# Moving the seven separately carried rows of a Winograd convolution from a store to a load

## The chip, the cores and the metric

The kernel runs on one core of a Trainium2 chip. The metric is the device time of one execution in microseconds (us). A measurement of this kernel is the median of several runs.

## What is computed

A 3x3 convolution with zero padding of one pixel, over 16 images of 64 channels and 64x64 points, to 128 output channels, all in float32. Cut to what matters, the reference is:

```python
x_pad = np.pad(x, ((0, 0), (0, 0), (1, 1), (1, 1)), mode='constant')
# for every image b, output channel co, input channel ci, and kh, kw in 0..2:
output[b, co] += weight[co, ci, kh, kw] * x_pad[b, ci, kh:kh+h, kw:kw+w]
```

The input is 16.8 MB, the weights 0.3 MB, the output 33.6 MB.

## The kernel before

**Tiling.** Images are taken in eight pairs, p = 0 to 7: the 64 channels of two images fill the 128 partitions, so that one pair is a tile of 128 partitions by 64 rows by 64 columns of float32 (16 KB in each partition, 2 MB in all). Every pair is computed in two halves of 32 output rows. For each half, `transforms` (L135) makes float16 sums, differences and outer differences of rows (`sums` L110, `diffs` L117, `outers` L124), on VectorE for the very first half and on GpSimd for all others, two halves ahead of their use. `cast` (L130) makes a float16 copy of 17 rows on ScalarE, one half ahead. TensorE then runs 54 matmuls of 64 by 128 weights on up to 512 columns (L170), into eight PSUM tiles. ScalarE copies some of them out (L192, L253), and VectorE adds and subtracts the rest into the output tile (L247, L249, L251).

**Homes.** Tiles in SBUF have fixed places. `X_HOME` (L49) gives the place of each input pair: pairs 0, 1 and 2 in slots s0, s1 and s2, pairs 3 and 4 side by side in the double slot "d", pair 5 in s2 again, pairs 6 and 7 in "d" again. `O_HOME` (L50) gives that of the two output images of each pair; pairs 0, 3 and 6 (`BOTH`, L51) use a double tile and are stored by one transfer of 4 MB (L207), the others by one transfer of 2 MB for each image (L216).

**Transfers.** All of them are issued by SyncE (SP in the profile), in the order of the program, on one queue that feeds 16 DMA engines. A transfer over 128 partitions gives each of the 16 engines eight partitions, so eight packets (16 for a double tile), one for each partition and tile, and a record of four bytes at its end, which counts its completion. The order is: weights (L59); pair 0 in two pieces, pair 1, pair 2 (all L67, from `load`, L62); pairs 3 and 4 together (L81); then, as computation finishes, the stores of pairs 0 and 1, the load of pair 5, the stores of pair 2, the load of pair 6, the store of pair 3, the load of pair 7, the stores of pairs 4, 5, 6 and 7. `NEXT_LOADS` (L53) places the loads. SyncE waits at each store for VectorE and ScalarE to have written the tile, at each late load for GpSimd and ScalarE to have read the slot's old contents.

**The seven rows.** `FEW = 5, 1, 7` (L52) names pair 5, image 1, seven rows. In `store` (L204) this one image of the sixth pair is carried in three transfers instead of one: rows 0 to 56 from all 128 partitions (L213), rows 57 to 63 from partitions 0 to 123, and rows 57 to 63 from partitions 124 to 127. The second and third have 1792 bytes in each partition. In the trace their 128 packets lie on four of the 16 DMA engines, 32 on each. Every other transfer of the program lies evenly on all 16.

Of the kernel before, what the change touches and what calls it, by code (L numbers as in the profile page):

```python
# [15 lines left out]
def kernel(  # L16
# [12 lines left out]
    nc = tc.nc  # L29
    B, CI, H, W = x.shape  # L30
    CO = weight.shape[0]
# [4 lines left out]
    keep = tc.keep_in_program_order  # L36
    x_rows = x.rearrange("b c h w -> (b c) h w")
# [11 lines left out]
    X_HOME = [0, 1, 2, ("d", 0), ("d", 1), 2, ("d", 0), ("d", 1)]  # L49
    O_HOME = ["b", (3, 4), (0, 1), "b", (3, 4), (0, 1), "b", (2, 3)]  # L50
    BOTH = (0, 3, 6)  # L51
    FEW = 5, 1, 7  # L52
    NEXT_LOADS = {(1, 1): 5, (3, 0): 6, (4, 0): 7}  # L53

    def home(k, name):
        return slots.tile([128, H, W], F32, tag=f"s{k}", name=name)
# [3 lines left out]
    xs = {}  # L60

    def load(p, cuts=((0, H),)):  # L62
        if X_HOME[p] in range(5):
            xs[p] = home(X_HOME[p], "xs")
        for lo, hi in cuts:
            keep(
                nc.sync.dma_start(  # L67
                    xs[p][:, lo:hi, :], x_rows[128 * p : 128 * p + 128, lo:hi, :]
                )
            )  # L70

    two = slots.tile([128, 2, H, W], F32, tag="d", name="two")
    for p in range(NP):
        if X_HOME[p] not in range(5):
            xs[p] = two[:, X_HOME[p][1], :, :]

    load(0, ((0, 34), (34, H)))
    load(1)
    load(2)
    rows = x_rows[128 * 3 : 128 * 5, :, :].rearrange("(g p) h w -> p g h w", g=2)  # L80
    keep(nc.sync.dma_start(two, rows))  # L81
# [116 lines left out]
    def outputs(p):  # L198
        if O_HOME[p] == "b":
            both = slots.tile([128, 2, H, W], F32, tag="b", name="both")  # L200
            return both, [both[:, b2, :, :] for b2 in range(2)]
        return None, [home(k, "ot") for k in O_HOME[p]]

    def store(p, both, ots):  # L204
        if p in BOTH:
            pair = out[2 * p : 2 * p + 2, :, :, :].rearrange("b c h w -> c b h w")
            keep(nc.sync.dma_start(pair, both))  # L207
            return
        for b2 in range(2):
            parts = [(0, CO, 0, H)]  # L210
            if (p, b2) == FEW[:2]:
                at = H - FEW[2]
                parts = [(0, CO, 0, at), (0, 124, at, H), (124, 4, at, H)]  # L213
            for c, n, lo, hi in parts:
                keep(
                    nc.sync.dma_start(  # L216
                        out[2 * p + b2, c : c + n, lo:hi, :], ots[b2][c : c + n, lo:hi, :]
                    )
                )

    for n, (p, h) in enumerate(halves):
        if n + 2 < len(halves):
            tr[halves[n + 2]] = transforms(nc.gpsimd, *halves[n + 2])
        if h == 0:
            both, ots = outputs(p)
# [28 lines left out]
        if h == 1:  # L254
            store(p, both, ots)
# [32 lines left out]
```

## Time and profile before

| what | value |
|---|---|
| median of 3 runs | 127.15 us (126.87 to 127.34) |
| the profiled execution: its own time | 127.13 us |
| the profiled execution: its span | 125.4 us |
| last matmul group ends | 102.44 us |
| last store issued | from 103.18 us on |
| HBM read / written | 17.07 MB / 33.55 MB |
| mean DMA rate over the span | 405 GB/s |
| granted TensorE clock, mean | 0.917 |

The span is what the profile covers, from its first to its last instruction; the execution's own time holds 1.7 us more around it. All times of instructions and packets below are in us from the start of the span. The page of the profile shows for each engine how busy it was in 40 equal slices of 3.1 us; for the DMA line a digit of 9 means that the 16 DMA engines were busy for 90% of the slice or more. The view of windows gives the same for stretches that one chooses, with the mean rate in GB/s. A DMA share of 1.01 or 1.02 stands for "all 16 engines": successive packets of an engine overlap by some 4 ns.

### The profile page before, as it was taken

The numbers are of one execution on the slowest core, as the hardware profiler recorded it, in microseconds if no ns is written. First come the engines' busy times: TensorE is split into PE (matmuls) and PEld (weight loads), VectorE is DVE, ScalarE is ACT, GpSimd is POOL, SyncE is SP. The second block draws the span as 40 slices with busy tenths as digits, with TensorE's granted clock in tenths as the row PEclk, the third lists the DMA queues.
The fourth block names the chain that finished last, engine by engine and source line by source line (L and its number), as shares of the span: only waits on it lengthen the run. The fifth ranks groups of instructions, "written<-read, shape, count | busy, mean of one in ns | idle before, by whom it ended". The sixth has DMA issues, their size and how long they took to land.

```text
span 125.4 us, 2343 instructions
## 1 busy us (share of the span) xinstructions
PE 95.6 (76%) x873; PEld 48.9 (39%) x873; DVE 66.8 (53%) x104; ACT 85.4 (68%) x150; POOL 90.5 (72%) x52
## 2 busy tenths in 40 slices
PE   0349999999999999999999999999999960000000
PEld 0223555555455555555555555555555520000000
DVE  0199658393939476574939394765749390000000
ACT  4458598989797988989897979789898930000000
POOL 2209999999999999999999999999999300000000
PEclk9999999999999999999999999999999996555555
DMA  4999999999999999999999999999999999999971
GB/s 132 371 453 423 434 424 439 423 335 418 434 431 429 426 434 418 423 429 434 416 439 424 423 423 423 418 431 434 423 424 423 433 416 443 423 429 444 418 335 47
DMA packets 3827, 50.78 MB, mean 405 GB/s; under 512 B 360, under 2 KB 488, under 8 KB 744
## 3 DMA queue, kind: packets, MB, share of 16 engines
q1 hardware_dynamic: 3816, 50.63, 96.2%
q8 instruction: 7, 0.11, 0.3%
q14 instruction: 4, 0.03, 0.1%
HBM read 17.07 MB, written 33.55 MB: 404 GB/s over the span
## 4 chain that ended last, share of the span: by engine, by line
PE 76%; DMA 2%; DVE 2%; POOL 1%; DVEq 0%; ACT 0%; issue 0%
PE acc L170 75%; DMA w_raw<-in_weight_dram 2%; DVE ss L114 1%; DVE ot L251 1%; POOL w L87 1%; DVEq L283 0%; DVE th L141 0%; DVE Wt L142 0%; PE wp L102 0%; ACT g0h L139 0%; DVEq L142 0%
## 5 line engine op out<-in xcount | busy, mean ns | idle before, releaser
L170 PEld LDWEIGHTS <-Wt 64*128 64x128 f16 x864 | 48.0, 96 | 48.5 <-issue 3.0
L192 ACT COPY ut<-acc 128x512 f32<-128x512 f32 x96 | 48.7, 612 | 4.4 <-PE acc L170 4.4
L170 PE MATMUL acc<-xh,Wt 64*128 64x504 f16 (+3 forms) x384 | 46.2, 372 | 0.0
L170 PE MATMUL acc<-ss,Wt 64*128 64x504 f16 (+1 forms) x192 | 24.8, 392 | 2.3 <-DVE ss L114 2.3
L170 PE MATMUL acc<-ee,Wt 64*128 64x504 f16 (+1 forms) x192 | 26.4, 377 | 0.0
L247 DVE TENSOR_TENSOR ot<-acc,ut 128x512 f32<-128x512 f32 x20 | 12.9, 686 | 20.0 <-ACT ut L192 15.8
L114 POOL TENSOR_TENSOR ss<-xs 128x1024 f16<-128x1024 f32 x7 | 16.6, 2366 | 4.7 <-DMA xs<-in_x_dram 4.7
L127 POOL TENSOR_TENSOR ee<-two 128x1024 f16<-128x1024 f32 x8 | 19.0, 2378 | 0.0
L114 POOL TENSOR_TENSOR ss<-two 128x1024 f16<-128x1024 f32 x8 | 19.0, 2369 | 0.0
L127 POOL TENSOR_TENSOR ee<-xs 128x1024 f16<-128x1024 f32 x7 | 16.6, 2376 | 0.0
L253 ACT COPY ot<-acc 128x512 f32<-128x512 f32 x20 | 10.7, 589 | 5.5 <-PE acc L170 5.5
L170 PE MATMUL acc<-dd,Wt 64*128 64x504 f16 (+1 forms) x96 | 13.9, 392 | 0.0
L247 DVE TENSOR_TENSOR both<-acc,ut 128x512 f32<-128x512 f32 x12 | 7.7, 686 | 11.0 <-ACT ut L192 7.9
L251 DVE TENSOR_TENSOR ot<-ut,acc 128x512 f32<-128x512 f32 x20 | 12.8, 682 | 0.2
L249 DVE TENSOR_TENSOR ot<-acc,ut 128x512 f32<-128x512 f32 x20 | 12.8, 680 | 0.0
L121 POOL TENSOR_TENSOR dd<-two 128x512 f16<-128x512 f32 x8 | 10.3, 1287 | 0.0
L121 POOL TENSOR_TENSOR dd<-xs 128x512 f16<-128x512 f32 x7 | 10.0, 1423 | 0.0
L132 ACT CAST xh<-two 128x1088 f16<-128x1088 f32 x8 | 9.3, 1157 | 0.0
L132 ACT CAST xh<-xs 128x1088 f16<-128x1088 f32 x8 | 9.2, 1145 | 0.0
L253 ACT COPY both<-acc 128x512 f32<-128x512 f32 x12 | 6.4, 589 | 3.5 <-PE acc L170 3.5
L251 DVE TENSOR_TENSOR both<-ut,acc 128x512 f32<-128x512 f32 x12 | 7.7, 683 | 0.1
L249 DVE TENSOR_TENSOR both<-acc,ut 128x512 f32<-128x512 f32 x12 | 7.7, 680 | 0.0
(23 smaller groups left out, 14.9 us busy)
## 6 DMA issues: line engine op xcount, KB each, us to landing
out_dram<-ot SPq DMA_DIRECT2D x9, 2048.0 KB, 18.5
out_dram<-both SPq DMA_DIRECT2D x3, 4096.0 KB, 22.5
xs<-in_x_dram SPq DMA_DIRECT2D x3, 2048.0 KB, 16.2
two<-in_x_dram SPq DMA_DIRECT2D x1, 4096.0 KB, 28.4
two<-in_x_dram SPq DMA_DIRECT2D x2, 2048.0 KB, 23.1
out_dram<-ot SPq DMA_DIRECT2D x1, 1824.0 KB, 24.3
xs<-in_x_dram SPq DMA_DIRECT2D x1, 1088.0 KB, 5.4
xs<-in_x_dram SPq DMA_DIRECT2D x1, 960.0 KB, 7.4
```

The source lines that it names most:

```text
L87: keep(nc.gpsimd.tensor_copy(w16[:, 0, :], w_raw))
L114: keep(eng.tensor_add(t, v[:, j : j + 16, 0, :], v[:, j : j + 16, 1, :]))
L121: keep(eng.tensor_sub(t, v[:, j : j + RB, 1, :], v[:, j : j + RB, 0, :]))
L127: keep(eng.tensor_sub(t, xs[p][:, r - 1 : r + 15, :], xs[p][:, r + 1 : r + 17, :]))
L132: keep(nc.scalar.copy(t, xs[p][:, C_ROW[h] : C_ROW[h] + 17, :]))
L170: nc.tensor.matmul(tiles[b2][:, lo:hi, c_lo:c_hi], Wt[p0 : p0 + 64, wi, kw, :], src[p0 : p0 + 64, first : last + 1 : step, c_lo + kw - 1 : ...
L192: keep(nc.scalar.copy(ut, tiles[b2]))
L247: keep(nc.vector.tensor_add(ov[b2][:, jg : jg + RB, 1, :], pg2[b2], ug[b2]))
L249: keep(nc.vector.tensor_add(ov[b2][:, jf : jf + RB, 0, :], pf1[b2], uy[b2]))
L251: keep(nc.vector.tensor_sub(ov[b2][:, jf : jf + RB, 1, :], ux[b2], pf2[b2]))
L253: keep(nc.scalar.copy(ov[b2][:, jg : jg + RB, 0, :], pg1[b2]))
```

## The change

The split in three transfers is taken from the store of the sixth pair's second image and given to the load of the third pair (p = 2), as rows 0 to 56 over all partitions, rows 57 to 63 over partitions 0 to 123, and rows 57 to 63 over partitions 124 to 127. The store becomes one transfer of 2 MB. The number of transfers, the bytes and the number of packets stay as they are; so does every instruction of the compute engines, in kind and order.

```diff
-    FEW = 5, 1, 7
+    FEW = 2, 7
...
     def load(p, cuts=((0, H),)):
         if X_HOME[p] in range(5):
             xs[p] = home(X_HOME[p], "xs")
-        for lo, hi in cuts:
-            keep(
-                nc.sync.dma_start(
-                    xs[p][:, lo:hi, :], x_rows[128 * p : 128 * p + 128, lo:hi, :]
-                )
-            )
+        parts = [(0, 128, lo, hi) for lo, hi in cuts]
+        if p == FEW[0]:
+            at = H - FEW[1]
+            parts = [(0, 128, 0, at), (0, 124, at, H), (124, 4, at, H)]
+        for c, n, lo, hi in parts:
+            r = 128 * p + c
+            keep(nc.sync.dma_start(xs[p][c : c + n, lo:hi, :], x_rows[r : r + n, lo:hi, :]))
...
         for b2 in range(2):
-            parts = [(0, CO, 0, H)]
-            if (p, b2) == FEW[:2]:
-                at = H - FEW[2]
-                parts = [(0, CO, 0, at), (0, 124, at, H), (124, 4, at, H)]
-            for c, n, lo, hi in parts:
-                keep(
-                    nc.sync.dma_start(
-                        out[2 * p + b2, c : c + n, lo:hi, :], ots[b2][c : c + n, lo:hi, :]
-                    )
-                )
+            keep(nc.sync.dma_start(out[2 * p + b2, :, :, :], ots[b2]))
```

## The prediction

> **What bounds the kernel now.** I read the page first: the slices, the queues, the chain.
>
> ```profile
> PE   0349999999999999999999999999999960000000
> DMA  4999999999999999999999999999999999999971
> q1 hardware_dynamic: 3816, 50.63, 96.2%
> ```
>
> TensorE stops at slice 33, the DMA engines go on to slice 39. The chain of waits ends in a store of VectorE's last tile at 103 us and gives 75% to the matmuls; but the 22 us behind that are transfers alone. SyncE's own waits and the chain end tell why:
>
> ```profile
> SPq L283 <- DMA out_dram<-ot: 9.9, 3, 4.8
> ...
> SPq L283 <- DMA out_dram<-both: 9.6, 1, 9.6
> ...
> 102.44 0.68 DVE ot L251
> 103.12 0.60 DVEq L283
> ```
>
> After the last store is issued (103.18) the core only waits for stores issued before. So the queue is the bound, and the question is when its last engine is done. The view of windows at the end:
>
> ```profile
> 104.00:116.00 12.00, 0.00 (x0) 0.00 (x0) 0.00 (x0) 0.00 (x0) 0.00 (x0) 0.52 1.01 433
> ...
> 120.00:121.00 1.00, 0.00 (x0) 0.00 (x0) 0.00 (x0) 0.00 (x0) 0.00 (x0) 0.50 0.77 328
> 121.00:122.00 1.00, 0.00 (x0) 0.00 (x0) 0.00 (x0) 0.00 (x0) 0.00 (x0) 0.50 0.65 279
> 122.00:123.00 1.00, 0.00 (x0) 0.00 (x0) 0.00 (x0) 0.00 (x0) 0.00 (x0) 0.50 0.35 147
> 123.00:124.00 1.00, 0.00 (x0) 0.00 (x0) 0.00 (x0) 0.00 (x0) 0.00 (x0) 0.50 0.08 33
> ```
>
> The share falls from 1 to 0 over four microseconds: the engines end at different times, and the last one sets the end. No view lists engines, so I took the trace's packet records (start, duration, bytes) and joined each to the one that starts 4 ns before its end; that gives 16 unbroken chains. Where two packets end within a few ns the join can swap two engines; the counts of 1792-byte packets show it for one of the four engines below. What I read from the chains:
>
> - A 16384-byte packet takes 607 ns from start to start, one of 14592 bytes (57 rows) 541, one of 1792 bytes 70. There is no gap on any engine from 2 us to its end.
> - The four engines with 32 packets of 1792 bytes ("the four") end at about 122.0 to 122.9 (the swapped one), 122.60, 123.20 and 123.38; the other twelve between 120.18 and 124.17, the last two at 124.07 and 124.17. Then 1.2 us of end work make the span, 1.7 more the execution's 127.13, which is the median of the runs (127.15) but for 0.02.
> - The pieces of seven rows are what brings the four near the end: at the end of the big piece of that store they stand at 100.9 to 101.7, the two slowest others at 104.6 and 104.7.
>
> **The change part by part.**
>
> *Work for each engine.* Removed from the store and added to the load are the same packets. On each of the four: 32 x 70 = 2.24 us more, 8 x (607 - 541) = 0.53 us less; on each of the twelve 0.53 less. Over the whole run each engine's sum stays. Between the third pair's load (about 18 us) and the sixth pair's store (about 101 us) the four are now 1.71 us later than before and the twelve 0.53 earlier, 2.24 apart. That a read of 1792 bytes costs as a write, no row shows; the reads at hand go as fast as writes (8704 bytes 324 ns, so 27 bytes/ns, as for 16384), so I take 70; bounds 70 and 89, what a read packet of 2304 bytes took: 32 x 19 = 0.6 us more on the four.
>
> *Does an engine run dry?* The twelve reach each later transfer 0.53 us earlier. A packet starts 1.0 us after its issue (weights: 0.74, first packet 1.74). What was issued but not moved is the cover. Least at the store of pair 1 (34.14 + 1.0): moved are 35.14 us x 391 GB/s = 13.74 MB, issued before are 14.98 MB (weights 0.29, seven units of 2.097), so 1.24 MB or 2.9 us at 432 GB/s. Next least is the first store: 10.78 - 9.33 MB, 3.4 us. So 0.53 is covered; if it weren't, the gap would cost at most 0.53 on fast engines, which end up to 4 us before the last.
>
> *SyncE.* Two issues move ahead of the double load, at 0.3 to 0.45 us each: it is issued at 3.9 instead of 3.07, and served at 18. Nothing.
>
> *Readers of the rows.* GpSimd's sums of the second half of pair 2 and ScalarE's copy of it get two more waits, at 27.7 and 31.1. The pieces land at about 18.4 + 1.7 = 20.1. Nothing. Late loads of the four (pair 6, pair 7) come 1.7 us later: pair 7 on them at 82 to 84.5, GpSimd needs it at 86.46, nothing; and a delay in GpSimd has 7.6 us of queue (3.3 MB left at 104.18) before it touches the end.
>
> *Changeovers from loads to stores.* Here the order matters.
>
> ```profile
> 24.00:26.00 2.00, 2.00 (x22) 1.00 (x19) 0.82 (x2) 2.00 (x5) 2.00 (x3) 1.00 1.02 434
> 26.00:29.00 3.00, 3.00 (x32) 1.59 (x30) 2.90 (x5) 2.34 (x5) 3.00 (x2) 1.00 0.99 322
> 29.00:33.00 4.00, 4.00 (x42) 2.05 (x40) 2.15 (x4) 3.56 (x7) 4.00 (x3) 1.00 1.01 430
> ```
>
> Where the double load ends and the first store begins, the rate falls by a quarter with all engines "busy". In the chains fifteen engines end the load between 28.2 and 28.7 and lose 0.3 to 1.0 us each. The sixteenth shared its time with an instruction fetch at 21.25 (each of seven such fetches costs its engine about 1.3 us), was still loading when the others stored, had one packet of 2.15 us, and ended at 31.18: the end of its load before (18.21) + 16 x 0.607 + 1.3 would be 29.2, so it lost 1.95, some 1.0 more than the worst of the others. It is the engine that ends last, at 124.17. Again at pair 6's load: most engines end it at about 67.3 without loss; those that end later lose 1.13 (end 71.21), 0.56 (69.47), 0.24 and 0.19 (69.3, 68.9). At pair 5's and pair 7's loads late engines lose 0 to 0.5, without order. So reading late, beside others' writes, has cost 0 to 1.0 at the first changeover and, by lateness, about 0.33 us per us at the second.
>
> In the changed kernel the four end the double load at 29.2 to 29.8 instead of 27.5 to 28.1 before loss, with the twelve at 27.0 to 27.6: they stand where the sixteenth stood. Price at the first changeover 0 (pair 5's load) to 1.0 (the sixteenth); I take 0.5, since four late readers instead of one may share the loss. At pair 6 they are 2.7 us later than before against the rest: 0 to 1.1, taken by the slope as 1.0 for the engine of 123.38. Its end: 123.38 + 0.5 + 1.0 = 124.9, which passes 124.17 by 0.7: **127.13 + 0.73 = 127.9**. At the upper ends 123.38 + 1.0 + 1.1 = 125.5: 128.4.
>
> [...] In the four's pieces, packets of one engine go to 31 partitions, and partitions are otherwise shared out evenly. From 100 to 104 us, with the pieces in it, the mean rate is 424 GB/s against 433 behind it: 9 x 4 us = 36 KB, 0.08 us. [...]
>
> **Rivals.**
>
> 1. *The order doesn't matter: not slower.* If late reading costs nothing when four engines do it together (as at pair 5's load), every engine ends where it did: 127.1. It decides below 0.79 us in all on the engine of 123.38 (124.17 - 123.38); from there on the end moves. For it: no gap anywhere, equal sums, a smooth 426 to 430 GB/s from 29 to 60 us. Against it: the sixteenth engine.
> 2. *The two slowest gain.* They are among the twelve and reach the changeovers 0.53 earlier; if the company of four other late readers, or a changeover in two groups, spares both of them 0.8 us, the end falls to the four's 123.38: 127.13 - 0.79 = 126.3. Against it: both must gain, and the four must not lose.
> 3. *The twelve keep no relief* (partitions of other engines written by the four, the mechanism that I priced by the 100 to 104 us row, or pieces that don't go to four engines at all): the store then takes its full 0.53 us back, 124.17 + 0.53: 127.66. Against it: 0.08 us in that row, and 32 packets on each of four engines for the same shape in the store.
>
> **How the numbers follow.** 0.5% is 0.63 us, about what a measurement of this kernel can tell from no change. The forecast 127.9 (its own range 127.8 to 128.5) has 0.50; rival 1 0.31; rival 3 0.06; rival 2 0.13. So slower 0.50, same 0.31 + 0.06 = 0.37, faster 0.13. The range of 8 in 10: below it I leave rival 2 (0.13), so it starts at 126.9, rival 1 with the scatter of the runs (0.25 us); above it 0.07, upper ends at all changeovers and slow small reads (0.6): it ends at 128.6.
>
> **What would show it.** Right: four engines with their 1792-byte packets at about 18 us; GB/s in the windows 26 to 31 lower in sum than before, since the dip lasts longer; the four ending the double load at 30 or later; packets over 1 us on them there and at 68 to 72; at the end, the share at 124 to 125 above 0. Wrong: a dip as before and the four's engines at 122 to 123.4 (rival 1); the share at 123 to 124 at 0 (rival 2); all twelve 0.53 later at the end (rival 3). It would be wrong altogether if TensorE waited (its last matmul later than 103), since the cover of 7.6 us then shrinks.

## The result and the profile after

The changed kernel takes 128.22 us (median of 6 runs, 127.82 to 128.44) against 126.94 (126.81 to 127.34) of the kernel before in the same measurements: a ratio of 1.0087, 95% interval 1.0067 to 1.0108, so about 1.1 us slower (the two medians differ by 1.28). The profiled execution took 128.35 us with a span of 126.5, 1.1 more than before. The prediction was 127.9, slower, with a range from 126.9 to 128.6. Its number held; the traces and the experiments below show that the mechanism it gave for the number did not.

What bounds the kernel is the same. The page's slices after:

```profile
PE   0349999999999999999999999999999920000000
DMA  4999999999999999999999999999999999999970
GB/s 117 387 439 440 415 376 256 430 425 435 425 412 438 435 430 420 420 435 435 427 425 420 435 430 430 427 425 430 430 420 435 425 425 440 425 435 425 430 306 41
```

TensorE stops at slice 33 as before, the DMA engines work on to slice 39. New is a rate of 376 and 256 GB/s in the sixth and seventh slice (15.8 to 22.1 us), while the engines are shown as busy. The end of the chain (start, duration, what) and SyncE's own waits (total, times, longest) after:

```profile
101.85 0.68 DVE ot L243
102.53 0.60 DVEq L275
```
```profile
SPq L275 <- DMA out_dram<-ot: 12.0, 3, 4.8
SPq L275 <- DMA out_dram<-both: 9.6, 1, 9.6
```

Computation ends a little earlier than before (102.44), and what SyncE waits for at the end is stores alone: 12.0 + 9.6 us, where it was 9.9 + 9.6. Nothing that computes has lost time. The same windows at the end as before the change (columns: window, busy time and count of each engine, TensorE clock, DMA share, GB/s):

```profile
120.00:121.00 1.00, 0.00 (x0) 0.00 (x0) 0.00 (x0) 0.00 (x0) 0.00 (x0) 0.50 0.99 426
121.00:122.00 1.00, 0.00 (x0) 0.00 (x0) 0.00 (x0) 0.00 (x0) 0.00 (x0) 0.50 0.73 311
122.00:123.00 1.00, 0.00 (x0) 0.00 (x0) 0.00 (x0) 0.00 (x0) 0.00 (x0) 0.50 0.58 246
123.00:124.00 1.00, 0.00 (x0) 0.00 (x0) 0.00 (x0) 0.00 (x0) 0.00 (x0) 0.50 0.27 115
124.00:125.00 1.00, 0.00 (x0) 0.00 (x0) 0.00 (x0) 0.00 (x0) 0.00 (x0) 0.50 0.12 49
```

The slope has the same form and lies about one microsecond later. Joined into chains as in the prediction, the packets end at 122.97 on the mean of the 16 engines (122.14 before) and at 125.20 on the last (124.17). It isn't the four alone that are later. The records of four bytes that close each transfer keep the engines apart where the join can't: the four end at 123.70, 124.50, 124.68 and 124.82, about 1.5 us later than before, and the other twelve end 0.6 us later on the mean. One of these twelve is the last engine of all.

Where the time went is seen in two windows, which I use for all kernels below: 12 to 25.5 us, which holds the third pair's load and most of the double load, and 25.5 to 32 us, the changeover to the first store. Loss is (432 - rate) x length / 432, with 432 GB/s for 16 unhindered engines (16384 bytes in 607 ns on each); a packet that a window cuts makes it uncertain by about 0.1 us. Before, then after:

```profile
12.00:25.50 13.50, 13.50 (x127) 6.85 (x124) 8.39 (x14) 11.23 (x21) 13.50 (x8) 1.00 1.01 430
25.50:32.00 6.50, 6.50 (x65) 3.40 (x62) 4.55 (x8) 5.84 (x11) 6.50 (x4) 1.00 1.00 381
```
```profile
12.00:25.50 13.50, 13.50 (x130) 6.78 (x128) 8.89 (x15) 11.71 (x21) 13.50 (x8) 1.00 1.02 375
25.50:32.00 6.50, 6.50 (x66) 3.28 (x63) 4.55 (x8) 5.54 (x10) 6.50 (x4) 1.00 1.00 426
```

In the first window 57 x 13.5 / 432 = 1.78 us are lost, where 0.06 were; in the second 0.09, where 0.77 were. The balance is 1.72 - 0.68 = 1.04 us on the average of the engines; the last engine's end moved by 1.03, the mean of the ends by 0.83, and the span grew by 1.1. In the packet records the loss of the first window lies from 17.5 to 21.7 us, exactly while the 128 packets of 1792 bytes are under way. They took 74 ns each as stores, all of them; as loads 74 to 206, the median 131.5. And the packets of 16384 bytes beside them, on the other twelve engines, took 0.99 us on the median (up to 1.20) instead of 0.61.

So two questions were put to the chip: what makes the small pieces of a load so costly, for all engines; and why the loss at the changeover went away.

### The profile page after: what moved, and what is told of

It is laid out like the page before. It is cut to its first block, busy times and chain, and to the rows that moved or that the text cites. A ratio compares the mean times of both kernels' runs of the same rounds, so it can differ in the third digit from the quotient of the medians.

```text
span 126.5 us, 2346 instructions
## 1 busy us (share of the span) xinstructions
PE 94.8 (75%) x873; PEld 47.6 (38%) x873; DVE 66.5 (53%) x104; ACT 85.3 (67%) x150; POOL 90.6 (72%) x52
## 4 chain that ended last, share of the span: by engine, by line
PE 74%; DMA 2%; DVE 2%; POOL 1%; DVEq 0%; ACT 0%; issue 0%
PE acc L171 74%; DMA w_raw<-in_weight_dram 2%; DVE ss L115 1%; DVE ot L243 1%; POOL w L88 1%; DVEq L275 0%; DVE th L142 0%; DVE Wt L143 0%; PE wp L103 0%; ACT g0h L140 0%; DVEq L143 0%
## 5 line engine op out<-in xcount | busy, mean ns | idle before, releaser
L171 PEld LDWEIGHTS <-Wt 64*128 64x128 f16 x864 | 46.6, 95 | 49.1 <-issue 2.3
L239 DVE TENSOR_TENSOR ot<-acc,ut 128x512 f32<-128x512 f32 x20 | 12.9, 686 | 19.9 <-ACT ut L193 15.8
L171 PE MATMUL acc<-dd,Wt 64*128 64x504 f16 (+1 forms) x96 | 13.3, 380 | 0.0
## 6 DMA issues: line engine op xcount, KB each, us to landing
out_dram<-ot SPq DMA_DIRECT2D x10, 2048.0 KB, 22.1
```

The source lines that it names most:

```text
L171: nc.tensor.matmul(tiles[b2][:, lo:hi, c_lo:c_hi], Wt[p0 : p0 + 64, wi, kw, :], src[p0 : p0 + 64, first : last + 1 : step, c_lo + kw - 1 : ...
L239: keep(nc.vector.tensor_add(ov[b2][:, jg : jg + RB, 1, :], pg2[b2], ug[b2]))
```

## The experiments

Theories for the first: **H**, small reads of HBM at a pitch of 16 KB are slow; **S**, writes into SBUF by four engines, spread over partitions that other engines serve in the large transfers (32 of the pieces lie on each of the four, where a transfer over 128 partitions has eight packets on each of 16 engines), slow everything (S1: because of whose partitions they are; S2: because they are four engines with many small packets). For the second: **L**, the prediction's, that engines which read late at the changeover lose time; **C** and **D**, that the loss belongs to the changeover itself, or to all engines reaching it together; **V**, that an earlier loss takes its place. Edits are against the changed kernel if nothing else is said.

### One transfer of all 128 partitions for the seven rows

```diff
-            parts = [(0, 128, 0, at), (0, 124, at, H), (124, 4, at, H)]
+            parts = [(0, 128, 0, at), (0, 128, at, H)]
```

> The seven rows of pair 2 are loaded by one transfer over all 128 partitions, so 16 engines with eight 1792-byte packets each and no engine takes over another's partitions. Theory H (the reads of 1792 bytes at a pitch of 16 KB in HBM are slow): the rate around 18 us falls as in the changed kernel (some 0.7 MB less moved than at 432 GB/s), and the time is 128.3 or more, since the twelve engines lose their relief too. Theory S (four engines that write into partitions spread over all of SBUF slow each other and the rest): no dip at 18 us, 1792-byte packets at about 74 ns, and the time of a kernel without any split, 127.4 to 127.8. Theory L (the prediction: engines that read late at the changeover lose time): no dip at 18, the dip at 26 to 29 as before the change, 127.4 to 127.8.

Measured: 127.69 us, ratio 1.0020 (0.9987 to 1.0053). The 1792-byte packets took 74 to 85 ns. From 17 to 20 us the view of windows of this kernel says:

```profile
17.00:20.00 3.00, 3.00 (x32) 1.56 (x30) 1.05 (x3) 3.00 (x7) 3.00 (x3) 1.00 1.03 430
```

430 GB/s: the same bytes from the same places of HBM in pieces of the same size, and hardly a loss (0.19 us from 12 to 25.5). The loss at the changeover (25.5 to 32 us: 376 GB/s, 0.84 us) is there. H falls here.

### The same pieces from consecutive places of HBM

```diff
+            rows_in = x_rows[r : r + n, lo:hi, :]
+            if hi - lo == FEW[1]:
+                at_row = 128 * p * H + FEW[1] * c
+                flat = x_rows.rearrange("r h w -> (r h) w")
+                rows_in = flat[at_row : at_row + FEW[1] * n, :].rearrange("(r h) w -> r h w", h=FEW[1])
```

> As the changed kernel, with the same three transfers on the same engines into the same partitions, but the two small ones read 1792-byte pieces that lie one behind the other in HBM (other input rows, so rows 57 to 63 of pair 2 are replaced by other data). Theory H: no dip at 18 us, 1792-byte packets at 74 ns, time 127.0 to 127.4. Theory S: dip as in the changed kernel, 128.2. Theory L: no matter for the order, 127.8 to 128.4, with the loss at 26 to 31.

Measured: 127.97 us, ratio 1.0046 (1.0015 to 1.0077).

```profile
12.00:25.50 13.50, 13.50 (x129) 6.79 (x127) 8.72 (x14) 11.36 (x22) 13.50 (x7) 1.00 1.01 379
25.50:32.00 6.50, 6.50 (x64) 3.33 (x62) 4.55 (x9) 5.84 (x10) 6.50 (x5) 1.00 1.01 431
```

The loss while the pieces are loaded is there (1.66 us, packets up to 225 ns) though nothing is left of the pitch: H falls a second time. The time lies between the changed kernel's and the kernel's without a split.

### No split at all

```diff
-    FEW = 2, 7
+    FEW = 8, 7
```

> No transfer is split: pair 2 is loaded whole and all images are stored whole. H, S and L alike: no dip at 18 us, the dip at 26 to 29 as before the change (322 GB/s), the twelve engines end 0.53 us later than before the change and the four 1.7 earlier: 127.4 to 127.8. It is the level from which the worth of the split in the store (before) and its cost in the load (after) are counted.

Measured: 127.66 us, ratio 1.0024 (0.9996 to 1.0052), no loss at 18 us (430 GB/s from 12 to 25.5), 0.84 us at the changeover (376). That is as expected of all theories. The split in the store was worth about 0.3 us to the kernel before, at the edge of what this measurement shows; the split in the load costs against no split some 0.8.

### The pieces within SBUF, without HBM

Pair 2 is loaded whole; the two transfers copy seven rows of pair 0 into a spare tile.

```diff
+            for c, n in ((0, 124), (124, 4)):
+                keep(nc.sync.dma_start(spare[c : c + n, :, :], xs[0][c : c + n, 0 : FEW[1], :]))
```

> Pair 2 is loaded whole; at the same place of the queue two transfers of 124 and 4 partitions copy seven rows of pair 0 from SBUF to a spare tile in SBUF, on the same four engines, 1792 bytes in each partition, without HBM (extra work that the output does not use; the store is whole). Theory S: a dip at 18 to 22 us as in the changed kernel. Theory H: none, 1792-byte packets at about 74 ns. Time under H: the twelve as without any split, 127.4 to 127.8; under S about 1.0 more.

Measured: 129.08 us (2 runs), ratio 1.0137 (1.0043 to 1.0231).

```profile
12.00:25.50 13.50, 13.50 (x130) 6.93 (x128) 8.72 (x15) 11.53 (x21) 13.50 (x8) 1.00 1.00 363
25.50:32.00 6.50, 6.50 (x66) 3.35 (x64) 4.55 (x9) 5.79 (x10) 6.50 (x4) 1.00 1.03 439
```

2.2 us lost ahead, packets of 74 to 216 ns with a median of 129, as in the changed kernel, with no read of HBM in the pieces at all. This is S. The time is 0.3 us above the range that S had. The changeover is again free of loss.

### The pieces within HBM, without SBUF

Pair 2 is loaded whole; the same seven rows are copied to a place of the output in HBM that the last store overwrites.

```diff
+            for c, n in ((0, 124), (124, 4)):
+                r = 128 * p + c
+                keep(nc.sync.dma_start(out[15, c : c + n, at:H, :], x_rows[r : r + n, at:H, :]))
```

> Pair 2 is loaded whole, all stores are whole; at the same place of the queue two transfers of 124 and 4 partitions copy the seven rows from HBM to a place in HBM that a later store overwrites (extra work): the same four engines, the same small reads, no write into SBUF. Theory S (writes into SBUF by four engines): no dip at 18 us. The four engines are then 2.24 us behind the other twelve at the changeover at 26 to 29. Theory L (reading late costs): the loss there is as large as before the change or larger, time 127.5 to 128.4. Theory D (the loss at 26 to 29, 0.75 us, comes from all 16 engines changing over together, and is gone when four of them are late): no dip there either, and the end of the twelve 0.75 earlier than without any split: 126.7 to 127.1.

Measured: 128.91 us, ratio 1.0125 (1.0081 to 1.0169), later than any theory had it.

```profile
12.00:25.50 13.50, 13.50 (x130) 6.84 (x127) 8.50 (x14) 11.43 (x21) 13.50 (x8) 1.00 1.02 420
25.50:32.00 6.50, 6.50 (x66) 3.35 (x62) 4.55 (x9) 5.84 (x10) 6.50 (x4) 1.00 0.96 360
```

While the pieces run 0.38 us are lost, against 1.78 in the changed kernel: without writes into SBUF the great loss is gone, as S has it. At the changeover 1.08 us are lost, somewhat more than without any split (0.84), though four engines end the double load 2.6 to 4.2 us after most others: D falls, four late engines alone don't take the loss away. The pieces held their four engines for 4.3 us (packets up to 0.67 us), and those end late; the time is theirs and says little of the others.

### All 16 engines alike, but 64 partitions at a time

```diff
-            parts = [(0, 128, 0, at), (0, 124, at, H), (124, 4, at, H)]
+            parts = [(0, 128, 0, at), (0, 64, at, H), (64, 64, at, H)]
```

> The seven rows of pair 2 are loaded by two transfers of 64 partitions each. [...] Theory S1 (what slows is that engines write into partitions that are others' in the large transfers): a dip at 18 us, its size not known, at least a third of the 1.8 us of the changed kernel. Theory S2 (what slows is four engines with 32 small packets each in a row): no dip, as with one transfer over 128 partitions (127.4 to 127.8).

Measured: 127.85 us (2 runs), ratio 1.0050 (1.0012 to 1.0088).

```profile
17.00:20.00 3.00, 3.00 (x32) 1.54 (x30) 1.05 (x3) 3.00 (x7) 3.00 (x3) 1.00 1.02 330
```

330 GB/s where the transfer over 128 partitions had 430: the packets are as many, as large and as evenly spread over the engines; what differs is that each transfer writes into one half of the partitions (and that it is one transfer more). From 12 to 25.5 us 0.84 us are lost, 47% of the changed kernel's. So S2 can't be all of it: the 64 partitions at a time, or the one transfer more, have a part at least. Whether that part is S1 is not shown. The trace names no partition of a packet; that a transfer over 64 partitions is shared out among the engines otherwise than one over 128, so that engines write into partitions of others, was my assumption in expecting the dip. Nor does this run part it from another form: that what slows is all 16 engines writing into one half of the partitions at a time. Whether the use of four engines adds the rest of the changed kernel's loss is not shown either. The changeover is almost free of loss again (421 GB/s, 0.17 us).

### The pieces where stores follow: pair 7, and the end of the loads

```diff
-    FEW = 2, 7
+    FEW = 7, 7
```

> The split in 128, 124 and 4 partitions is in the load of pair 7 instead of pair 2, so that stores follow behind the pieces and not another load. If four engines' writes into SBUF slow only other writes into SBUF (theory S, contention on the way into SBUF): the twelve are reading SBUF for the store of pair 4 by then, no dip or under 0.3 us around 80 us, 1792-byte packets at 74 to 80 ns, time as before the change, 126.8 to 127.3. If they slow every transfer: a dip of some 1.8 us at 80, time 128.2 to 128.8.

Measured: 127.32 us, ratio 1.0014 (0.9984 to 1.0043); packets 74 ns on the median, up to 168. Around the load, in this kernel and in the kernel before:

```profile
78.00:87.00 9.00, 9.00 (x88) 4.59 (x86) 6.85 (x12) 7.68 (x14) 9.00 (x6) 1.00 1.01 410
```
```profile
78.00:87.00 9.00, 9.00 (x88) 4.60 (x86) 6.40 (x11) 7.68 (x15) 9.00 (x6) 1.00 1.01 425
```

0.46 us lost against 0.15: a small price, where the same pieces ahead of another load lost 1.7. The second kernel puts them at the end of the first loads (split in two transfers for pairs 3 and 4), with the first store behind:

```diff
-    keep(nc.sync.dma_start(two, rows))
+    keep(nc.sync.dma_start(two[:, 0, :, :], rows[:, 0, :, :]))
+    for c, n, lo, hi in ((0, 128, 0, at), (0, 124, at, H), (124, 4, at, H)):
+        keep(nc.sync.dma_start(two[c : c + n, 1, lo:hi, :], rows[c : c + n, 1, lo:hi, :]))
```

> Pairs 3 and 4 are loaded by two transfers instead of one, the second of them split in 128, 124 and 4 partitions; the other loads and all stores are whole. The pieces lie at the very end of the loads, ahead of the first store. Theory S: the twelve go on with the store, so no dip from the pieces. With theory D, the loss of 0.75 us at 26 to 29 goes too: 126.2 to 126.6, faster than both kernels. Without D: 126.8 to 127.3, as before the change. With theory L: 127.8 to 128.4.

Measured: 127.41 us, ratio 1.0027 (1.0000 to 1.0054); packets 74 ns on the median. From 25.5 to 32 us:

```profile
25.50:32.00 6.50, 6.50 (x65) 3.33 (x63) 4.55 (x8) 5.84 (x11) 6.50 (x5) 1.00 0.95 355
```

1.16 us at the changeover, 0.3 more than without a split, and no gain. As S has it, the pieces cost little once the other engines read SBUF for a store instead of writing into it. The hope behind D fails once more.

### Three and fourteen rows

`FEW = 2, 3` and `FEW = 2, 14` instead of `FEW = 2, 7`.

> As the changed kernel with three rows carried separately instead of seven (768 bytes in each partition). Theory S (writes into others' partitions slow all engines, by the bytes): a dip at 18 us of 3/7 of 1.8, so 0.75 us. For the dip at 26 to 29 two theories. C (it belongs to the changeover and is as large as without any split): 0.75 there too, time 127.4 - 0.2 + 0.75 = 128.0 to 128.3. V (a loss of some 0.8 us in the loads comes once, and an earlier loss takes its place): 0 to 0.3 there, time 127.4 to 127.7.

> As the changed kernel with fourteen rows carried separately (3584 bytes in each partition). Theory S by the bytes: a dip of 3.5 us from 17 to about 25 us, none at 26 to 29, and the end 1.2 (the twelve, which get 0.53 more relief) to 3.0 us (the four) later than in the changed kernel: 129.4 to 131.3. If the price were one for each of the pieces' 128 packets: a dip of 1.8 us as with seven rows.

Measured: three rows 127.76 us, ratio 1.0049 (1.0023 to 1.0075); fourteen 132.18 (2 runs), ratio 1.0400 (1.0372 to 1.0427). The two windows, for three and then for fourteen:

```profile
12.00:25.50 13.50, 13.50 (x130) 6.04 (x126) 9.19 (x15) 11.69 (x22) 13.50 (x7) 1.00 1.00 410
25.50:32.00 6.50, 6.50 (x64) 3.00 (x62) 4.55 (x8) 5.61 (x10) 6.50 (x5) 1.00 1.00 423
```
```profile
12.00:25.50 13.50, 13.50 (x122) 6.60 (x120) 8.18 (x13) 10.78 (x20) 13.50 (x7) 1.00 1.02 317
25.50:32.00 6.50, 6.50 (x66) 3.31 (x62) 4.22 (x7) 5.84 (x12) 6.50 (x5) 1.00 1.00 416
```

0.69, 1.78 and 3.59 us for 0.10, 0.23 and 0.46 MB: it goes by the bytes, not by the packets, at 3.0 to 3.4 times what the bytes would take at 432 GB/s. At the changeover three rows leave 0.14 us, so a loss of 0.7 ahead takes the place of the 0.8 there: that speaks for V, though the time is a little above what V had. With fourteen rows the time is 0.9 above the range that was expected; the profiled execution's last engine ends 3.7 us later than in the changed kernel, where 1.8 are the larger loss and most of the rest is the four engines' own work (32 packets of 3584 bytes each).

### A longer row of loads

No split, and one more load ahead of the first store.

```diff
+    spare = const.tile([128, 28, W], F32)
+    keep(nc.sync.dma_start(spare, x_rows[896:1024, 0:28, :]))
```

> No transfer is split; behind the double load, ahead of the first store, one more load of 28 rows over 128 partitions into a spare tile (0.9 MB, 2.1 us of the queue, not used by the output). Theory C (the dip at 26 to 29 belongs to the changeover from loads to stores): it moves to 27.6 to 31. Theory V (it comes after some 25 us of loads, wherever the stores begin): it stays at 25.5 to 28.5, size 0.8. Time in both: that without any split and 2.1 more, 129.5 to 129.9.

Measured: 129.37 us (2 runs), ratio 1.0179 (1.0152 to 1.0206).

```profile
25.50:32.00 6.50, 6.50 (x64) 3.40 (x62) 3.87 (x7) 5.84 (x12) 6.50 (x5) 1.00 1.00 391
27.00:31.00 4.00, 4.00 (x40) 2.09 (x38) 2.91 (x5) 3.34 (x7) 4.00 (x3) 1.00 1.00 368
```

The dip has moved: in the packet records from 25.5 to 28.5 us without the load to 27.7 to 30.5 with it, and it is 0.6 us. So the place of the loss is the changeover (C), not a time or a number of bytes. Together with the runs above: it belongs to the changeover, it is there with and without four late engines, and it is nearly gone (0 to 0.24 us) in all seven kernels in which pieces had slowed the writes into SBUF before it. Why, stays open.

### The split in the store and a small disturbance ahead

The kernel before, with the last three rows of pair 2 loaded in transfers of 64 partitions, to buy the loss at the changeover off with a smaller one.

```diff
+        if p == 2:
+            parts = [(0, 128, 0, H - 3), (0, 64, H - 3, H), (64, 64, H - 3, H)]
```

> The kernel before, with its split in the store, and besides the last three rows of pair 2 loaded by two transfers of 64 partitions each (768 bytes in each partition, even on all 16 engines). Theory S1 by the bytes: a dip at 18 us of 3/7 of the 0.8 us that seven rows in transfers of 64 cost, so 0.3 to 0.4. Theory V: the loss at the changeover at 26 to 29 falls to 0.1 to 0.3 in exchange, time 126.6 to 127.1, at best a little below the kernel before. Theory C: the loss there stays at 0.75, time 127.3 to 127.6.

Measured: 127.38 us, ratio 1.0022 (1.0008 to 1.0037), so a little slower than the kernel before.

```profile
12.00:25.50 13.50, 13.50 (x128) 6.91 (x126) 8.53 (x14) 11.47 (x22) 13.50 (x7) 1.00 1.01 424
25.50:32.00 6.50, 6.50 (x66) 3.35 (x64) 4.55 (x8) 5.84 (x11) 6.50 (x5) 1.00 1.00 416
```

The exchange works in the windows, 0.25 and 0.24 us instead of 0.06 and 0.77, so 0.34 less. The time doesn't follow, it is where C had it: the engines of the profiled execution end at 122.13 on the mean (122.14 before the change). Some of the 0.34 is in its first six microseconds, which lost 0.2 more than before's, the rest in small dips later. One profile can't tell whether that is chance. None of the kernels tried is faster than the kernel before.

## Why the prediction came out, step by step

- **What bounds the kernel, and no engine running dry**: right. TensorE and the stores' issue end as before, GpSimd waits for no late load, the queue holds until the end.
- **The price of the pieces**, "I take 70; bounds 70 and 89": wrong, and the largest miss. As loads ahead of loads they took 131.5 ns on the median, and the packets of the twelve other engines 0.99 us in place of 0.61 for some 4 us: 1.78 us lost on the average of all 16, where the prediction had 2.24 us of the four's own work and no loss for the rest.
- **The twelve 0.53 us earlier**, from the third pair's load on: it did not come. They had lost more than that by 21.7 us.
- **Changeovers**, "0 to 1.0; I take 0.5": wrong in sign. The four end the double load at 31.2 to 31.7, over 2 us after most others, as foreseen, and neither they nor the rest lose there: 0.09 us in place of 0.77. No packet beyond 0.66 us lies at 68 to 72 either. The sixteenth engine of the kernel before was one engine, and I made a rule of it.
- **The end**, "the engine of 123.38 becomes the last": wrong, though nearly so in number. The four that end the double load at 31.2 to 31.7 have 152 packets of 0.607 us still to move, 92.3 us, so none of them can end before 123.5; by the records they end at 123.70 to 124.82, close to the forecast 124.9. What made them late is mostly the price of the pieces; behind the double load they lose another 0.6 to 0.7 us each on the average, in single packets, and none of it at pair 6's load. The last engine of all, at 125.20, is one of the twelve. It ends the double load at 29.09, and its store packets take about 0.65 us instead of 0.61 until some 100 us. The kernel before has such an engine too; there it ends at 124.07. The prediction took no account of it, and why it is slow stays open.
- **The signs it named**: two of those for "right" came, the four ending the double load at 30 or later and a share above 0 at 124 to 125 (0.12). The first came from the pieces, the second from the four and the slow engine of the line above. The two that would have shown the mechanism, a lower rate at 26 to 31 and packets over 1 us there and at 68 to 72, did not.
- **Rival 3, with its partitions of other engines written by the four**: the nearest to what happened, and I gave it 0.06. The row that I held against it (100 to 104 us, 0.08 us lost) was of a store. For stores that row stands; for loads the pieces do take the other engines' time (0.99 us on the median for a packet of 16384 bytes instead of 0.61). Rival 3 had the relief of 0.53 us taken back. Measured are 1.72 us more lost than before from 12 to 25.5 us, which it doesn't give.
- **The number**: +0.73 was forecast from 0.5 + 1.0 on one engine less its distance to the last (124.88 - 124.17 is 0.71, and the slope of 0.33 on 2.7 us is 0.9, which changes little); +1.1 came, from +1.72 at the pieces and -0.68 at the changeover on all engines. That both lie close is chance.

## What to carry to other kernels

A split of a transfer that does little harm as a store (0.08 us lost from 100 to 104 us in the kernel before) can cost several times its own length as a load (1.78 us lost here, 3.4 times what the bytes would take at 432 GB/s): keep loads that run beside other loads in one transfer over all 128 partitions, the form that lost least here (0.06 us with all rows in one, 0.19 with the seven rows in a second one), and put odd-sized pieces where the other engines read SBUF (0.46 us lost around pair 7's load, against 0.15 without the pieces). A price that is taken from a row of the other direction should keep the whole range open, and a rule of one late engine is no rule. When all engines are "busy", look at GB/s in short windows: both losses of this case, 0.8 and 1.8 us, show there and nowhere else on the page.

## What the runs showed of the hardware that was not expected

- Pieces of 124 and 4 partitions written into SBUF while the other engines write there too slow all 16 engines, to 219 to 260 GB/s from 19 to 22 us for seven rows; the loss goes by the bytes (0.69, 1.78, 3.59 us for 3, 7, 14 rows), whether they come from HBM or from SBUF (1.78 and 2.2 us for seven rows); read out of SBUF for a store they cost 74 ns a packet and 0.08 us beside (424 GB/s from 100 to 104 us in the kernel before). Two transfers of 64 partitions have 47% of that price (0.84 us).
- Where the long row of loads on all engines turns to stores, 0.6 to 1.1 us are lost for all of them; the loss moves with the changeover (from 25.5 to 28.5 us to 27.7 to 30.5 us behind one more load), and it is nearly gone (0.24 us or less) when such pieces have slowed the loads before. The cause is open.
- An instruction fetch of 16 KB costs the DMA engine that it falls on 1.3 to 1.4 us (one transfer's time on that engine less its usual time), seven times in a run; in the changed kernel each falls on another engine.
- One engine of the 16 takes about 0.65 us for a store packet of 16384 bytes instead of 0.61, from the first store to some 100 us, in the kernel before and in the changed one. It ends 0.1 us before the last engine there and is the last here. Its loads take the usual time. The cause is open.
